# Rounding of one expert's down weights placed behind the router's scores and the sorted list of experts

## The chip, the cores and the metric

The kernel runs on one core of a Trainium2 chip. The metric is the device time of that core in microseconds (us), as the median of several executions. Engines carry the profile's names: PE is TensorE, PEld its weight load, DVE is VectorE, ACT is ScalarE, POOL is GpSimd and SP is SyncE, which here only issues transfers.

## The reference

One layer of a diffusion backbone: 512 latent tokens and 256 context tokens of width 1024 pass a gated linear attention mixer; then a mixture of 16 experts follows, of which every token takes two. Cut to the part that matters here:

```
x = x + g1 * y                                   # y: the mixer's output
h2 = modulate(rmsnorm(x, norm2_g), sh2, sc2)
scores = sigmoid(h2 @ w_router); sel = scores + b_router
# the best of 4 groups of 4 experts (by its two highest), and in it the top 2 experts
gates = one_hot(top2) * scores / sum(scores of the two)
for e in range(16):
    he = silu(h2 @ w1[e]) * (h2 @ w3[e])         # 1024 -> 512
    out = out + gates[:, e] * (he @ w2[e])       # 512 -> 1024, the "down" product
x = x + g2 * out; return rmsnorm(x, final_g)
```

All inputs are float32.

## The kernel before

A program orders each engine's instructions: a list scheduler takes the traced instructions by priority and readiness in a simulation, unless a block is marked as a manual schedule (those keep the written order among themselves, and others may be put between them). Inside `with tc.issue_after(i)` every instruction on i's engine is put behind i on that engine; it is an order on that queue, not a wait on another engine.

Around the change there are four stages. First, the mixer's output projection (`oproj` in `project(n)`, for four blocks of 128 tokens): float32 products as three fp32r products (`mm3`, lines 51 to 53) of a rounded part and a rest. `second(n)` adds the residual (lines 717 and 718) and squares (719), `turn` transposes a block on PE (725) and copies it (727), `logits` multiplies by the router (732). Second, the scores: `score` (854), `add_bias` (857), the sigmoid's exponential on ACT (904, named `scored`), its rest on DVE, then 11 filler products on PE (`warm`, 912) while DVE works out the top two (924 to 941, result `ohs`). Third, PE counts (943 to 947), DVE makes one-hot rows `hot` (956), and `collect` (964) multiplies them with the residual stream to gather the tokens of expert 0, which gets its first 128 tokens that way; meanwhile DVE sorts experts 2 to 15 by load (1042 to 1052, the last is `eidl`) and writes the normalised tokens to memory for the gathers of the others (`scaled`, `normed`, 839 and 842). This stretch up to `collect` is one manual schedule over DVE, ACT, POOL and PE. Fourth, the experts: 0 and 1 always run, the rest in the order of the sorted list. Expert 0's gate and up products (line 1181) use raw float32 weights; its down product goes through `conv`: ACT casts a 128x1024 tile of weights to fp32r (`S.copy`, line 56), DVE subtracts to get the rest (`V.tensor_sub`, line 57), and PE takes both. There are three pairs of buffers for such halves (`wh`/`wl` twice and `fx`), used in turn, so that the down product's four tiles take three pairs and then the first again. Expert 1's gate and up tiles (line 1256) already stand behind `scored` and `eidl`.

Weights of 1 MB a tile come by SP's queue (`load_unit`, line 688), each into the next free buffer; `release` hands a buffer back and `pump` issues the next load. Experts' tokens come by indirect transfers on POOL (1102) and results are added to memory by others (1106).

Of the kernel before, what the change touches and what calls it, by code (L numbers as in the profile page):

```python
# [32 lines left out]
def dit_kernel(ctx: ExitStack, tc: tile.TileContext, I, out):  # L33
# [21 lines left out]
    def split(hi, lo, full):  # L55
        S.copy(hi, full)  # L56
        return V.tensor_sub(lo, full, hi.bitcast(F32))  # L57
# [17 lines left out]
    cc = glt("cc", [2, 8])  # L75
# [200 lines left out]
    def conv(st):  # L276
        w = cvs.pop(0)
        cvs.append(w)
        if halves[0]:
            for k in range(2):  # L280
                S.copy(w[0][:, k], st[:, k])  # L281
                mark[0] = V.tensor_sub(w[1][:, k], st[:, k], w[0][:, k].bitcast(F32))  # L282
        else:
            mark[0] = split(w[0], w[1], st)
        return w
# [413 lines left out]
    def release(u, *us):  # L699
        free.extend(u.pop(s) for s in us)  # L700
        pump()
# [39 lines left out]
    for k2 in range(4):  # L741
        w = first[k2] if k2 < 2 else wconv(2 * k2)
# [11 lines left out]
    w = [wconv(8), wconv(10)]  # L754
# [149 lines left out]
    scored = [S.activation(sc, lg, AF.Exp, scale=-1.0)]  # L904
# [334 lines left out]
    class Expert:  # L1239
# [32 lines left out]
        def down(s, u):  # L1272
            s.turn()
            for kt in range(4):
                w = u[4 + kt // 2][:, kt % 2 * D:kt % 2 * D + D]
                if not s.raw:
                    ws = conv(w.rearrange("p (a n) -> p a n", a=2))
                for t in s.tls:
                    t.dn(kt, w if isinstance(t, Part) else ws)
                if kt % 2:  # L1280
                    release(u, 4 + kt // 2)
            if s is not ex[0]:
                s.store()
# [112 lines left out]
    with tc.manual_schedule(engines={G.engine}):  # L1396
        ex = [Expert(cols[order[0]], True)]
# [23 lines left out]
    with tc.manual_schedule(engines=tail):  # L1421
        p_, q_ = ex[NE - 2:]
        p, q = p_.tls[0], q_.tls[0]
# [69 lines left out]
    n = nc.values_load(nblk[0:1, 0:1], min_val=0, max_val=NB)  # L1493
# [46 lines left out]
```

## Time and profile before

| what | value |
|---|---|
| median of 3 runs | 656.51 us (656.42 to 659.3) |
| profiled execution, its own time | 656.5 us |
| its span, first to last instruction | 654.7 us |
| PE busy | 599.0 us (91%) |
| DVE busy | 463.6 us (71%) |
| ACT busy | 302.6 us (46%) |
| transfers | 168.41 MB, mean 257 GB/s |

1.8 us of the profiled execution lie outside its span. A busy PE is not a PE at its peak: the row on the granted clock tells whether it ran at 2.4 or at 1.2 GHz.

### The profile page before, as it was taken

The page shows a single profiled execution, that of the slowest core. Times are in us where ns is not written, and L with a number is a line of the kernel's source. Part 1 is how long each engine was busy: PE and PEld are TensorE (multiplying, and loading weights), DVE is VectorE, ACT ScalarE, POOL GpSimd, SP SyncE. Part 2 cuts the span into 40 slices and gives each one's busy share as a digit, 9 for nine tenths or more (in the row PEclk, how much of TensorE's full clock was granted, in tenths as well). Part 3 has the DMA queues.
Part 4 walks back from the last instruction along what each step waited for, and adds up shares of the span by engine and source line. Part 5 has one row for each costly group of instructions (what it writes and reads, how often), then busy time and mean ns, then how long its engine had stood idle before and what let it go on. Part 6 is the DMA issues. An engine that isn't in the chain of part 4 may idle for free. (4 is left out here: it accounts for less than half of the span.)

```text
span 654.7 us, 11203 instructions
## 1 busy us (share of the span) xinstructions
PE 599.0 (91%) x4200; PEld 412.4 (63%) x4200; DVE 463.6 (71%) x984; ACT 302.6 (46%) x511; POOL 98.3 (15%) x102
## 2 busy tenths in 40 slices
PE   3999999999999999999979989999999999999741
PEld 2778577776878878778748465545565657664310
DVE  5667499849985972575288399465767689999615
ACT  6433399257352233642451255334444457773131
POOL 4030000010100010012200330120322222222032
PEclk9999999999999999999998999999999999999975
DMA  8996472220234861658662989899999999999974
GB/s 269 340 353 218 175 274 66 67 66 4 67 130 158 270 232 51 254 183 354 237 227 74 373 316 366 326 342 351 412 387 395 362 352 358 393 383 345 298 273 189
DMA packets 50251, 168.41 MB, mean 257 GB/s; under 512 B 6779, under 2 KB 17237, under 8 KB 37138
## 3 DMA queue, kind: packets, MB, share of 16 engines
q1 hardware_dynamic: 43216, 156.26, 64.4%
q0 software_dynamic: 5024, 8.70, 5.6%
q10 hardware_dynamic: 1954, 2.71, 1.3%
q8 instruction: 34, 0.56, 0.3%
q14 instruction: 23, 0.19, 0.1%
HBM read 158.64 MB, written 12.30 MB: 261 GB/s over the span
## 5 line engine op out<-in xcount | busy, mean ns | idle before, releaser
L51 PE MATMUL bk<-wh,fh 128*128 128x512 f32 (+3 forms) x276 | 110.9, 409 | 0.7 <-ACT fh L56 0.4
L52 PE MATMUL bk<-wl,fh 128*128 128x512 f32 (+3 forms) x276 | 111.3, 405 | 0.0
L53 PE MATMUL bk<-wh,fl 128*128 128x512 f32 (+3 forms) x276 | 109.0, 399 | 0.5 <-DVE fl L57 0.5
L282 DVE TENSOR_TENSOR wl<-st,wh 128x512 fp32r<-128x512 f32 x60 | 39.9, 685 | 38.9 <-ACT wh L281 37.6
L56 ACT CAST wh<-su 128x1024 fp32r<-128x1024 f32 x45 | 46.8, 1047 | 39.9 <-PE bk L53 38.7
L281 ACT CAST wh<-st 128x512 fp32r<-128x512 f32 x60 | 35.9, 620 | 59.5 <-PE bk L53 50.8
L51 PEld LDWEIGHTS bk<-wh,fh 128*128 128x128 f32 (+3 forms) x276 | 50.2, 183 | 19.2 <-ACT wh L56 3.3
L57 DVE TENSOR_TENSOR wl<-su,wh 128x1024 fp32r<-128x1024 f32 x45 | 54.5, 1222 | 10.5 <-ACT wh L56 8.3
L1106 POOL DMA_INDIRECT accd<-y,gix x16 | 37.2, 2324 | 164.8 <-DVE y L1166 78.2
L52 PEld LDWEIGHTS bk<-wl,fh 128*128 128x128 f32 (+3 forms) x276 | 50.6, 183 | 16.5 <-issue 3.3
L53 PEld LDWEIGHTS bk<-wh,fl 128*128 128x128 f32 (+3 forms) x276 | 50.6, 183 | 13.7 <-issue 1.2
L1202 PE MATMUL bk<-su,he 128*64 128x512 f32 (+1 forms) x136 | 21.7, 526 | 12.5 <-DMA su<-in_w_down_e_dram 9.6
L1202 PE MATMUL bk<-su,xg 128*32 128x256 f32 (+1 forms) x216 | 31.7, 485 | 1.5 <-DVE xg L1196 1.5
L56 ACT CAST fx<-su 128x1024 fp32r<-128x1024 f32 x21 | 22.0, 1050 | 21.8 <-PE bk L53 21.6
L57 DVE TENSOR_TENSOR fx<-su,fx 128x1024 fp32r<-128x1024 f32 x21 | 25.7, 1222 | 7.4 <-ACT fx L56 7.2
L51 PE MATMUL bk<-fx,fh 128*128 128x512 f32 (+3 forms) x68 | 27.9, 410 | 1.2 <-ACT fh L56 1.2
L52 PE MATMUL bk<-fx,fh 128*128 128x512 f32 (+3 forms) x68 | 27.3, 402 | 1.0 <-DVE fx L57 1.0
L53 PE MATMUL bk<-fx,fl 128*128 128x512 f32 (+3 forms) x68 | 26.6, 394 | 0.2 <-DVE fl L57 0.2
L1102 POOL DMA_INDIRECT xg<-h2d,gix x16 | 20.1, 1259 | 39.2 <-DVE pis L1005 15.1
L250 POOL DMA_DIRECT2D mrd<-mrow x8 | 3.8, 487 | 129.2 <-DVE mrow L248 129.2
L1202 PEld LDWEIGHTS bk<-su,he 128*64 128x64 f32 (+1 forms) x136 | 6.6, 127 | 24.4 <-DMA su<-in_w_down_e_dram 11.0
L57 DVE TENSOR_TENSOR fl<-bk,fh 128x512 fp32r<-128x512 f32 (+3 forms) x25 | 15.5, 634 | 7.5 <-ACT fh L56 5.5
(476 smaller groups left out, 1303.6 us busy)
## 6 DMA issues: line engine op xcount, KB each, us to landing
su<-in_w_up_e_dram SPq DMA_DIRECT2D x23, 1024.0 KB, 8.2
su<-in_w_down_e_dram SPq DMA_DIRECT2D x21, 1024.0 KB, 7.8
su<-in_w_gate_e_dram SPq DMA_DIRECT2D x19, 1024.0 KB, 8.3
st<-in_gla_w_in_dram SPq DMA_DIRECT2D x10, 1024.0 KB, 5.0
QQ<-in_w_mod_dram SPq DMA_DIRECT2D x5, 1024.0 KB, 10.8
st<-in_w_gate_e_dram SPq DMA_DIRECT2D x5, 1024.0 KB, 6.8
st<-in_w_up_e_dram SPq DMA_DIRECT2D x5, 1024.0 KB, 9.0
B<-in_w_mod_dram SPq DMA_DIRECT2D x4, 1024.0 KB, 5.1
```

The lines of the kernel that those rows point to most:

```text
L51: PE.matmul(o, ah, bh, start=first, stop=False)
L52: PE.matmul(o, ah, bl, start=False, stop=False)
L53: return PE.matmul(o, al, bh, start=False, stop=last)
L56: S.copy(hi, full)
L57: return V.tensor_sub(lo, full, hi.bitcast(F32))
L250: G.dma_start(mrd[4 * h_ + c4:4 * h_ + c4 + 1, :], mrow[32 * c4:32 * c4 + 1, :])
L281: S.copy(w[0][:, k], st[:, k])
L282: mark[0] = V.tensor_sub(w[1][:, k], st[:, k], w[0][:, k].bitcast(F32))
L1102: G.indirect_dma_start(out=xg, out_offset=None, in_=src, in_offset=bass.IndirectOffsetOnAxis(ap=idx, axis=0), bounds_check=n - 1, oob_is_e ...
L1106: G.indirect_dma_start(out=dst, out_offset=bass.IndirectOffsetOnAxis(ap=idx, axis=0), in_=y, in_offset=None, bounds_check=n - 1, oob_is_er ...
L1202: PE.matmul(o[s.w * a:s.w * a + s.w], l, r(a), start=first, stop=last, tile_position=(0, s.w * a))
```

## The change

Expert 0 is `ex[0]`. The four conversions of its down weights are now traced inside two `issue_after` blocks: the four casts on ACT stand behind `scored` (line 904) on ACT's queue, the four subtractions on DVE behind `eidl` (line 1052) on DVE's queue. Nothing else is edited.

```diff
             for kt in range(4):
                 w = u[4 + kt // 2][:, kt % 2 * D:kt % 2 * D + D]
                 if not s.raw:
-                    ws = conv(w.rearrange("p (a n) -> p a n", a=2))
+                    with ExitStack() as cc:
+                        if s is ex[0]:
+                            for i in [scored[0], eidl]:
+                                cc.enter_context(tc.issue_after(i.ins))
+                        ws = conv(w.rearrange("p (a n) -> p a n", a=2))
                 for t in s.tls:
                     t.dn(kt, w if isinstance(t, Part) else ws)
```

## Rows read from the trace of the kernel before

**Rows 1.** The page: granted clock in 40 slices; one costly group (busy, mean ns).

```profile
PEclk9999999999999999999998999999999999999975
...
L56 ACT CAST wh<-su 128x1024 fp32r<-128x1024 f32 x45 | 46.8, 1047 | 39.9 <-PE bk L53 38.7
```

**Rows 2.** PE's timeline: start, duration, then [idle before <- what ended it].

```profile
327.61 0.40 PE L53 MATMUL bk<-wh,fx 128*128 128x512 f32 x1
...
336.06 0.40 PE L53 MATMUL bk<-wh,fx 128*128 128x512 f32 x1
...
341.12 0.63 PE L725 MATMUL bk<-ident,srg 128*128 128x128 f32 x4 [3.72 <-DVE srg L718]
...
343.12 1.89 PE L854 MATMUL bk<-sel,he 128*128 128x16 f32 x8
344.85 4.81 PE L912 MATMUL bk<-fh 128*128 128x512 f32 x11
349.70 0.20 PE L943 MATMUL bk<-ohs,tri 128*128 128x64 bf16 x1
...
350.76 7.51 PE L964 MATMUL bk<-hot,srg 128*128 128x128 f32 x64
...
380.45 1.07 PE L1136 MATMUL bk<-ident,xg 128*128 128x128 f32 x8
```

**Rows 3.** DVE's timeline ahead of the scores.

```profile
328.04 0.69 DVE L717 TENSOR_TENSOR srg<-bk,g1b 128x512 f32<-128x512 f32 x1 [0.26 <-PE bk L53]
328.76 0.69 DVE L718 TENSOR_TENSOR srg<-srg,su 128x512 f32<-128x512 f32 x1
...
335.69 1.22 DVE L57 TENSOR_TENSOR wl<-su,wh 128x1024 fp32r<-128x1024 f32 x1
...
337.35 1.23 DVE L57 TENSOR_TENSOR fx<-su,fx 128x1024 fp32r<-128x1024 f32 x1
...
338.56 0.68 DVE L717 TENSOR_TENSOR srg<-bk,g1b 128x512 f32<-128x512 f32 x1
339.16 1.22 DVE L57 TENSOR_TENSOR wl<-su,wh 128x1024 fp32r<-128x1024 f32 x1
340.29 0.69 DVE L718 TENSOR_TENSOR srg<-srg,su 128x512 f32<-128x512 f32 x1
```

**Rows 4.** ACT's timeline: the sigmoid's exponential and what comes next.

```profile
345.32 0.26 ACT L904 ACTIVATE sc<-lg 128x64 f32<-128x64 f32 x1 [1.79 <-DVE lg L857]
354.74 1.51 ACT L967 ACTIVATE full<-bk,m2T 128x128 f32<-128x128 f32 x4 [9.16 <-PE bk L964]
```

**Rows 5.** DVE's timeline from the list's last instruction to expert 0's end.

```profile
355.52 0.18 DVE L1052 CAST eid<-eidf 128x14 int32<-128x14 f32 x1
...
365.53 0.69 DVE L991 TENSOR_TENSOR ohx<-iot,zp 128x512 bf16<-128x512 bf16 x1
372.40 0.69 DVE L1148 TENSOR_TENSOR he<-he,bk 128x512 f32<-128x512 f32 x1 [6.18 <-PE bk L1181]
```

**Rows 6.** Windows: length, each engine's busy time, clock, DMA share, GB/s.

```profile
341.00:343.00 2.00, 1.45 (x20) 0.78 (x20) 1.21 (x4) 1.22 (x4) 0.00 (x0) 0.86 0.99 346
347.00:349.00 2.00, 2.00 (x6) 1.52 (x6) 1.97 (x11) 0.00 (x0) 0.00 (x0) 0.50 0.22 94
349.00:351.00 2.00, 1.83 (x15) 0.91 (x13) 1.47 (x8) 0.00 (x0) 0.00 (x0) 0.93 0.00 0
382.00:386.00 4.00, 3.52 (x21) 2.54 (x21) 4.00 (x22) 0.93 (x2) 0.95 (x1) 1.00 0.58 238
560.00:580.00 20.00, 19.70 (x99) 13.06 (x98) 19.54 (x32) 15.07 (x18) 5.98 (x2) 1.00 1.02 388
```

**Rows 7.** DVE's timeline near the end: one operation beside POOL's, and alone.

```profile
636.24 2.18 DVE L1351 TENSOR_TENSOR su<-B,srg 128x1024 f32<-128x1024 f32 x1 [5.54 <-DMA su<-accd]
642.62 1.22 DVE L1351 TENSOR_TENSOR su<-su,srg 128x1024 f32<-128x1024 f32 x1
```

**Rows 8.** POOL's timeline: the gather of expert 1's tokens, behind the gates.

```profile
368.87 1.10 POOL L1102 DMA_INDIRECT xg<-h2d,gix  x1 [2.59 <-DMA h2d<-xg]
```

## Prediction, made before the result was known

> **What bounds the kernel now.** I read the page first, for where TensorE does not have its clock: the row of the granted clock has nines almost throughout, an 8 in the slice from 344 to 360 us, and less at the very end [rows 1]. The slice with the 8 is the stretch of the scores, where the change lies, so I read the timelines of the engines there, and last the windows, to see what limits the stages behind it.
>
> Before the scores PE runs the output projection without a pause, and its last product starts at 336.06. Then it has nothing until 341.12: a pause of 3.72 us, ended by the residual addition (line 718) on DVE [rows 2]. The reader is to see in DVE's timeline why: DVE is not late with that addition because its input is late. It is busy with three subtractions of 1.22 us (line 57), which belong to expert 0's down weights, and these are wanted only some 35 us later. They stand among the small steps of the last token block: one at 335.69, one at 337.35 ahead of the product of line 717, and one at 339.16 between line 717 and line 718 [rows 3].
>
> From there a chain with no slack leads to the experts: addition, transposes, router products, scores (343.12), bias, exponential (345.32), the choice of the top two on DVE, the counts on PE (349.70), the collecting of expert 0's tokens (350.76) [rows 2 to 4]. PE's filler products run from 344.85 for 4.81 us, that is to 349.66, and end just when the counts can start, so they cost nothing [rows 2].
>
> **What the change takes from the path.** The three subtractions and their three casts leave this stretch. In the second token block, where nothing is put between, the product of line 717 starts at 328.04 after a last product that began at 327.61, 0.43 us later, and line 718 follows at 328.76, 0.72 us after line 717 [rows 2, 3]. By that pattern the last block's line 717 starts at 336.06 + 0.43 = 336.49 in place of 338.56, which is 2.07 us; and line 718 follows 0.72 us later in place of 340.29 - 338.56 = 1.73 us, which is 1.01 us. Together 3.08 us, and everything that hangs on line 718 moves by it. DVE is free by then: from 335.69 to 338.56 it has 2.87 us, of which the two subtractions are 2.45, so other work is 0.42 us, which fits into the 0.80 us from 335.69 to 336.49 [rows 3].
>
> **What it adds elsewhere: the casts.** ACT has 9.16 us without work behind the exponential until PE's collecting is ready [rows 4]. Three casts of 1.05 us [rows 1] take 3.1 us of it. Cost: nothing. If that cover were gone, they would cost their 3.1 us; but it would have to shrink by 6 us first. The fourth cast goes into a buffer pair that the first tile's products must leave first, so it stays where it was, during the down product.
>
> **The subtractions.** They now stand behind the list's last instruction, at 355.52 [rows 5]. Between that and expert 0's result DVE has a hole: its last small step starts at 365.53 and the next at 372.40 waits 6.18 us for PE [rows 5]. Three subtractions are 3.67 us, so they fit with 2.5 us to spare even if all else comes first. In which order the scheduler puts them is open. If they go ahead of the writes of the normalised tokens, the gather behind these writes is at most 3.67 us late against the rest; it starts at 368.87 [rows 8], and PE takes up its rows at 380.45 [rows 2], 11.6 us later, so a delay of that size has room. I take nothing; the other bound is the whole 3.67 us, if they miss the hole.
>
> A row near the end shows what POOL does to such an operation: a 128x1024 DVE product of two SBUF tensors took 2.18 us while POOL ran the same operation beside it and 1.22 us alone [rows 7]. The gates run on POOL ahead of the gather at 368.87 [rows 8], in just the stretch to which the subtractions go. The rule that stands behind this row: the Trainium skill, "SBUF — State Buffer", section "Who interferes with whom", says that a DVE instruction with two SBUF inputs and a GpSimd instruction that reads SBUF exclude one another, and the trace agrees with it by 2.18 against 1.22 us. By the rule the subtractions would be the slower the more gates they meet, which is the third rival below; without it they cost nothing.
>
> **The clock.** The fall and the rise lie inside the stretch: in the window from 341 to 343 us the mean clock is 0.86, which puts the fall to half (1.2 GHz) at 343 - 2 x 0.14 / 0.5 = 342.44; from 349 to 351 it is 0.93, which puts the rise at 349.28 [rows 6]. What PE did before the fall was the pause of 3.72 us and some short products; before the rise 4.4 us of filler products without a pause [rows 2]. With the pause cut to some 0.6 us (3.72 - 3.08) the scores may run at 2.4 GHz: their 1.89 us [rows 2] would be halved at best, so this gains 0 to 0.9 us. But then the fillers would end sooner too, and PE would stand idle ahead of the counts: at full speed 4.81 us become about 2.4, so a pause of 2.4 us, or less if the scores gained nothing. If the clock falls in that pause, collecting (7.51 us at full clock) starts slow, and as the rise came after 4.4 us of steady work, half of these, 2.2 us, are lost at most. So the clock's term lies between +0.9 and -2.2 us. The pause with a fall behind it was 3.72 us and the new one is 2.4, nearer to that than to none, so I count with a fall, but as it would come after part of the collecting or be over in part of it, with the smaller share: +0.4 for the scores and -0.4 for the collecting, nothing in sum. Both ends are kept.
>
> **Does it reach the end?** The stages behind are held either by PE or DVE or by transfers, and all of them start from this chain. Right behind expert 0, from 382 to 386, DVE is busy all of the 4 us and transfers only 0.58 [rows 6]: the engines set the pace. Later, as from 560 to 580, transfers are at 1.02 and PE at 19.70 of 20 [rows 6]: both. The loads that fill this stage go into buffers that the collecting and expert 0 free, so they move forward with them. I see nothing in the expert stage that is tied to an earlier time, so the 3.1 us should last: 656.5 - 3.1 = 653.4 us, from the profiled execution's own time, which is the median too (656.51).
>
> **The rivals.**
>
> *Clock lost in collecting.* The new pause ahead of the counts brings the fall to the collecting. Price up to 2.2 us, so a gain of 0.9 to 2.2: 654.3 to 655.6. For it speaks that a fall did come here [rows 6]; against it that the work ahead of the pause is denser than before.
>
> *Subtractions too late (slower).* The scheduler puts them behind the steps that wait for expert 0's result at 372.40. Then the down product waits for the first of them, and the rest fall into the stretch where DVE is full [rows 6], so up to 3.67 us are paid. The point from which it decides is 3.1 us: if all three miss the hole, 656.5 - 3.1 + 3.7 = 657.1, slower than before; with some of the reordering's own loss up to 659. Against it: they are ready long before, and DVE sits idle for 6.18 us [rows 5].
>
> *POOL in the way.* By the doubled duration of [rows 7] three subtractions would take 3 x 2.18 = 6.54 us for a hole of 6.18: 0.4 us lost, 653.8. Against it: the gates are small tensors, and each subtraction would have to meet one that is as long as itself.
>
> *Gain absorbed.* The transfers, at 1.02 from 560 on [rows 6], set the end whatever PE does before, or a new order of instructions in the experts gives it back: 656.5. Against it: they wait for buffers that are freed earlier. The change cannot fail to act at all, since the order on the queue is fixed by it, unless other work fills the holes; I see none.
>
> *More than that.* The clock does not fall at all and the later stages order themselves better: 652.4 or less.
>
> **How the numbers follow.** Forecast, 652.4 to 654.2 around 653.4: 0.55. Clock lost: 0.14. Subtractions late: 0.09. POOL: 0.05. Absorbed: 0.09. More: 0.08. The range must leave out no more than two in ten: it goes from 652.0, which leaves half of the last case out, to 656.6, which leaves out the late case. 0.5% is 3.3 us, about what a measurement of this kernel can tell from no change, so the line lies at 653.2, just inside the forecast. Of the forecast a bit under half lies below it, 0.25; all of "more" is 0.08; and 0.05 is for sizes that I took too low in the other cases: 0.38 faster. Slower by over 0.5% is above 659.8, which only a bad new order of the later stages gives, on top of the late case (0.02) or in place of "absorbed" (0.04): 0.06. The rest, 0.56, is the same.
>
> **What would show it.** In the changed trace line 57 has no instruction between 335 and 345; PE's pause of 3.72 us is below 1; line 718 follows line 717 after 0.72 us; the exponential starts near 342.2 or up to 0.9 earlier; three casts lie right behind it on ACT; three subtractions lie between 352.4 and 369.3 on DVE; collecting starts near 347.7 and takes 7.5 us at full clock, up to 9.7 if the fall is there; line 1148 starts near 369.3, and the down product behind it has no wait for line 57. I am wrong if the down product waits for a subtraction, if collecting runs at 1.2 GHz for long, or if the 3 us are there at 369 and gone by 400.

## The result, and the profile after

The change makes the kernel a little faster: 653.35 us median (650.64 to 657.62, 20 runs) against 657.18 us (653.83 to 661.07, 20 runs), a ratio of 0.995 with a 95% interval of 0.9929 to 0.9971. By the ratio that is 3.3 us, between 1.9 and 4.7; the two medians themselves differ by 3.83.

The profiled execution of the changed kernel has a span of 655.1 us, 0.4 more than the one before. Whoever compares these two numbers alone would call the change a loss, so the traces are compared by stretches.

DVE's timeline of the changed kernel, at the last token block and then behind the sorted list:

```profile
337.66 0.69 DVE L717 TENSOR_TENSOR srg<-bk,g1b 128x512 f32<-128x512 f32 x1
338.39 0.69 DVE L718 TENSOR_TENSOR srg<-srg,su 128x512 f32<-128x512 f32 x1
...
353.00 0.17 DVE L1052 CAST eid<-eidf 128x14 int32<-128x14 f32 x1
...
358.41 1.22 DVE L57 TENSOR_TENSOR fx<-su,fx 128x1024 fp32r<-128x1024 f32 x1
...
361.67 1.19 DVE L57 TENSOR_TENSOR wl<-su,wh 128x1024 fp32r<-128x1024 f32 x1
362.78 0.98 DVE L1071 TENSOR_TENSOR big<-zk,perm 128x784 f32<-128x784 f32 x1
363.68 1.21 DVE L57 TENSOR_TENSOR wl<-su,wh 128x1024 fp32r<-128x1024 f32 x1
...
369.88 0.69 DVE L1148 TENSOR_TENSOR he<-he,bk 128x512 f32<-128x512 f32 x1 [2.77 <-PE bk L1181]
```

Line 718 follows line 717 after 0.73 us, where it took 1.73 [rows 3], and the three subtractions stand behind the list, among the steps of the ranking (line 1071 is one). The hole ahead of expert 0's result has shrunk from 6.18 us [rows 5] to 2.77: the work moved into it, and nothing of it is late.

PE's timeline of the changed kernel:

```profile
337.23 0.40 PE L53 MATMUL bk<-wh,fx 128*128 128x512 f32 x1
...
339.22 0.63 PE L725 MATMUL bk<-ident,srg 128*128 128x128 f32 x4 [0.66 <-DVE srg L718]
...
341.22 1.29 PE L854 MATMUL bk<-sel,he 128*128 128x16 f32 x8 [0.16 <-DVE he L895]
342.35 4.14 PE L912 MATMUL bk<-fh 128*128 128x512 f32 x11
347.19 0.19 PE L943 MATMUL bk<-ohs,tri 128*128 128x64 bf16 x1 [0.71 <-DVE ohs L941]
...
348.24 7.51 PE L964 MATMUL bk<-hot,srg 128*128 128x128 f32 x64
...
355.79 13.98 PE L1181 MATMUL bk<-su,full 128*128 128x512 f32 x32
...
371.96 0.50 PE L51 MATMUL bk<-fx,fh 128*128 128x512 f32 x1 [0.68 <-ACT fh L56]
372.30 0.39 PE L52 MATMUL bk<-fx,fh 128*128 128x512 f32 x1
...
377.94 1.07 PE L1136 MATMUL bk<-ident,xg 128*128 128x128 f32 x8
```

The first products of expert 0's down weights (371.96 and 372.30) follow each other without a wait for a subtraction. The same timeline of the kernel before, two rows that were not shown, and then the changed kernel's row that answers to the second:

```profile
358.31 13.98 PE L1181 MATMUL bk<-su,full 128*128 128x512 f32 x32
...
601.39 3.65 PE L1202 MATMUL bk<-srg,xg 128*64 128x512 f32 x16
```

```profile
599.02 3.65 PE L1202 MATMUL bk<-srg,xg 128*64 128x512 f32 x16
```

PE's pause of 3.72 us [rows 2] is 0.66. From the last projection product to expert 0's first product (line 1181) the changed kernel takes 355.79 - 337.23 = 18.56 us, the one before took 358.31 - 336.06 = 22.25: 3.69 us less. The 0.4 us of the two spans is the sum of four stretches: the profiled execution of the changed kernel came to the last projection product 1.17 us later, in code that the change does not touch (a second execution of the same program, below, came there at 335.35, 0.71 us earlier than the kernel before); then 3.69 gained; then 243.23 in place of 243.08 us to the row of line 1202, 0.15 lost; and 56.08 in place of 53.31 us to the end, 2.77 lost. The experiments show that only the 3.69 belongs to the change.

ACT's timeline of the changed kernel, with the three casts behind the exponential:

```profile
342.82 0.26 ACT L904 ACTIVATE sc<-lg 128x64 f32<-128x64 f32 x1 [1.42 <-DVE lg L857]
342.98 1.03 ACT L56 CAST fx<-su 128x1024 fp32r<-128x1024 f32 x1
343.91 1.99 ACT L56 CAST wh<-su 128x1024 fp32r<-128x1024 f32 x2
352.22 1.51 ACT L967 ACTIVATE full<-bk,m2T 128x128 f32<-128x128 f32 x4 [6.32 <-PE bk L964]
```

6.32 us of the 9.16 [rows 4] are still free behind them.

### The profile page after: what moved, and what is told of

It is laid out like the page before. It is cut to its first block, busy times and chain, and to the rows that moved or that the text cites. A ratio compares the mean times of both kernels' runs of the same rounds, so it can differ in the third digit from the quotient of the medians.

```text
span 655.1 us, 11203 instructions
## 1 busy us (share of the span) xinstructions
PE 597.5 (91%) x4200; PEld 410.9 (63%) x4200; DVE 463.5 (71%) x984; ACT 302.9 (46%) x511; POOL 101.2 (15%) x102
```

## The experiments

One table for all, read from PE's timelines of one profiled execution each. "To collecting" is from the start of the last projection product to the start of line 964; "collecting" is that line's duration; "experts" is from the first product of line 1181 to the row of line 1202 shown above; "rest" from there to the end of the span. The ratio is to the kernel before, timed on the same chip; its median was 657.08 to 657.50 us there.

| kernel | to collecting | collecting | experts | rest | median us | ratio (95%) |
|---|---|---|---|---|---|---|
| before | 14.70 | 7.51 | 243.08 | 53.3 | 657.18 | |
| changed | 11.01 | 7.51 | 243.23 | 56.1 | 653.35 | 0.995 (0.9929 to 0.9971) |
| changed, again | 11.19 | 8.24 | 243.05 | 52.5 | 653.42 | 0.9941 (0.9916 to 0.9966) |
| subtractions only | 11.22 | 8.24 | 243.23 | 54.6 | 653.84 | 0.995 (0.993 to 0.9969) |
| casts only | 14.39 | 8.41 | 243.15 | 55.0 | 657.37 | 1.0014 (0.9992 to 1.0036) |
| subtractions late | 11.09 | 8.56 | 246.35 | 51.2 | 656.24 | 0.9991 (0.997 to 1.0012) |
| three idle ones added | 15.62 | 7.51 | 243.24 | 53.0 | 657.32 | 0.9995 (0.9976 to 1.0014) |
| nine idle ones added | 23.26 | 7.51 | 243.21 | 54.7 | 665.69 | 1.0113 (1.0092 to 1.0134) |
| subtractions past the gates | 11.00 | 7.51 | 243.12 | 51.5 | 653.27 | 0.9935 (0.9912 to 0.9957) |
| no fillers | 11.22 | 8.27 | 243.18 | 54.8 | 655.02 | 0.9958 (0.9937 to 0.998) |
| more fillers | 11.00 | 7.51 | 243.20 | 52.5 | 653.34 | 0.9948 (0.9928 to 0.9967) |
| before, with fillers | 14.05 | 8.80 | 243.13 | 51.9 | 656.79, one execution | |

**The changed kernel again.**

> The changed kernel once more, beside the kernel before on one chip. Theory (three subtractions off the scores' chain, 3.1 us, and the scores at full clock, 0.6 us): from the last projection product's start to the start of collecting (line 964) 11.0 us, where the kernel before has 14.70; the time 3 to 4 us under the kernel before. Rival (transfers set the end, the gain stays inside): the same 11.0 us, but the time within 1 us of the kernel before.

It took 653.42 us, 3.9 us under the kernel before by the ratio, with 11.19 us to collecting. The rival, a gain that stays inside, is out. PE's timeline of this execution, from the counts on:

```profile
345.29 0.21 PE L943 MATMUL bk<-ohs,tri 128*128 128x64 bf16 x1 [2.25 <-DVE ohs L941]
...
346.54 8.24 PE L964 MATMUL bk<-hot,srg 128*128 128x128 f32 x64
```

Here collecting took 8.24 us, behind a pause of 2.25 us ahead of the counts; more on that below. The profiled execution of this run has a span of 650.4 us, of the same program as the 655.1 above; the rest behind line 1202 is 52.5 us in the one and 56.1 in the other. So the 2.77 us that the first profile lost there is a spread of that stretch and not the change's. Over all kernels the rest lies between 51.2 and 56.1 us, in no order that follows the edits.

**Only the subtractions moved.**

```diff
-                            for i in [scored[0], eidl]:
+                            for i in [eidl]:
```

> Only the subtractions behind the list; the casts stay in the projection as in the kernel before. Theory: the casts cost nothing where they were, so 11.0 us from the last projection product to collecting, and the time of the changed kernel within 0.5 us. Rival (the casts hold up ACT's copies and squares there, and part of the gain is theirs): 11.5 us or more.

11.22 us to collecting, where the changed kernel took 11.01 and 11.19, and 653.84 us. So the gain comes without moving the casts: where they stood in the projection they cost nothing that these numbers show.

**Only the casts moved.**

```diff
-                            for i in [scored[0], eidl]:
+                            for i in [scored[0]]:
```

> Only the casts behind the exponential; the subtractions are free to follow them, and the order of instructions puts them at three places of the top-two choice on DVE, ahead of the counts. Theory: what counts is that DVE's subtractions stand on the chain, wherever; the scores come 3.7 us earlier as in the changed kernel, the choice takes some 3 us longer, so 14 to 14.7 us from the last projection product to collecting and the time of the kernel before within 1 us. Rival (only the place ahead of the scores hurts, for its pause of PE): 11 to 12 us, and 2 us or more faster than before.

The time is that of the kernel before. DVE's timeline of this kernel shows the three subtractions in the choice of the top two:

```profile
344.34 1.22 DVE L57 TENSOR_TENSOR fx<-su,fx 128x1024 fp32r<-128x1024 f32 x1
...
346.88 1.22 DVE L57 TENSOR_TENSOR wl<-su,wh 128x1024 fp32r<-128x1024 f32 x1
...
348.30 1.22 DVE L57 TENSOR_TENSOR wl<-su,wh 128x1024 fp32r<-128x1024 f32 x1
...
350.38 0.23 DVE L941 SCALAR_TENSOR_TENSOR ohs<-rk,gr 128x64 bf16<-128x64 f32 x1
```

The scores come as early as in the changed kernel, and against the run that moved only the subtractions 14.39 - 11.22 = 3.2 us are lost again between them and the counts. So the half of the change that matters is the one on DVE, and its place must be behind the whole chain; behind the scores is not enough.

**The subtractions late.** They stand behind the subtraction that splits expert 0's own hidden rows, past the hole.

```diff
-                            for i in [scored[0], eidl]:
+                            for i in [scored[0], s.tls[0].fl0]:
...
-            split(s.hh, s.hl, pt)
+            s.fl0 = split(s.hh, s.hl, pt)
```

> The subtractions are put behind the one that splits expert 0's own hidden rows, so past the hole on DVE; casts as in the changed kernel. This is the prediction's slower rival made real. Theory: collecting starts as in the changed kernel (11.0 us), then the down product waits about 1.2 us for the first subtraction, and DVE, which is full behind it, pays 1.2 to 3.7 us in all; the time 1 to 4 us above the changed kernel. If the later stages have slack on DVE: under 0.5 us above it.

PE's timeline of this kernel, in the down product and at its end:

```profile
373.06 0.73 PE L51 MATMUL bk<-fx,fh 128*128 128x512 f32 x2 [0.68 <-ACT fh L56]
374.92 0.79 PE L52 MATMUL bk<-fx,fh 128*128 128x512 f32 x1 [1.12 <-DVE fx L57]
375.51 0.63 PE L53 MATMUL bk<-fx,fl 128*128 128x512 f32 x1
...
381.90 1.07 PE L1136 MATMUL bk<-ident,xg 128*128 128x128 f32 x8
```

and one of its windows (length, each engine's busy time, clock, DMA share, GB/s):

```profile
376.00:378.00 2.00, 2.00 (x6) 1.59 (x5) 1.13 (x1) 0.93 (x1) 0.00 (x0) 0.50 1.02 336
```

The down product waits 1.12 us for the first subtraction. Behind it the granted clock is at half, 0.50 in this window, and products of 0.40 us take up to 0.63; in the changed kernel it is 1.00 there. The experts' stretch is 246.35 us, some 3.2 more than in every other kernel, and the time is 656.24 us, 2.8 above the changed kernel. The slower rival costs what it was said to cost, 1 to 4 us, and takes the gain back, but only in part in the way that was said. From the start of the two products of line 51 to line 52 it takes 1.52 us more than in the changed kernel (1.86 against 0.34), which is the wait; from line 52 to line 1136 it takes 1.34 us more (6.98 against 5.64), and there the clock is low. Behind that only some 0.3 us are left for a full DVE.

**Idle subtractions added.** The changed kernel with subtractions of no use between lines 717 and 718 of the last block, three or nine (`k`); nothing reads their result.

```diff
-        V.tensor_mul(x1[:, n, sl], ps, g1b[:, sl])
+        V.tensor_mul(x1[:, n, sl], ps, g1b[:, sl]); [V.tensor_sub(cvs[1][1], *[f.rearrange("p (a n) -> p a n", a=2) for f in (a2b, sh2b)]) for _ in range(k if (n, hf) == (3, 1) else 0)]
```

> The changed kernel with three subtractions of no use (same form, 1.22 us each, other data) between lines 717 and 718 of the last token block. Theory (time on DVE at this place is all that counted): addition 3.67 us later, so about 14.7 us from the last projection product to collecting as in the kernel before, and its time within 1 us. Rival (the gain came from elsewhere, the order of casts or of the later stages): the time stays 2 us or more under the kernel before.

> The same with nine of them, 11.0 us. Theory (everything behind hangs on this chain): 22 us from the last projection product to collecting and the time 7 to 8 us above the kernel before, 11 above the changed kernel. Rival (transfers set the end and can catch up): 5 us or less above the kernel before.

DVE's timeline with nine:

```profile
336.90 11.28 DVE L717 TENSOR_TENSOR wl<-xg 128x1024 fp32r<-128x1024 f32 x9
348.10 0.68 DVE L718 TENSOR_TENSOR srg<-srg,su 128x512 f32<-128x512 f32 x1
```

Three bring the time of the kernel before back (0.9995), though they read and write other data. Nine take 11.28 us, cost 12.3 us to collecting against the changed kernel (23.26 - 11.01; the long pause takes PE's clock at the scores as well) and 12.3 us of time (665.69 - 653.35). Both are a little more than expected: 23.26 us where 22 was said, and 8.4 us above the kernel before (657.33 on that chip) where 7 to 8 was. To within what these times tell (6.0 to 8.8 us above the kernel before, for 23.26 - 14.70 = 8.56 us on the chain) a microsecond on this chain is a microsecond of the kernel, and no catching up by transfers can be seen. With three, "to collecting" is 0.9 us longer than before, where the same was expected. About half of it is the subtractions: in the kernel before only 3.08 of the 3.67 us lay on the chain, and nearly all of them do here (line 718 starts 4.69 us after the last projection product, 4.23 before). The other half is the clock: the transposes behind the longer pause of 4.19 us take 1.09 us, 0.63 before.

**The subtractions past the gates.** They stand behind the last step of the ranking, line 1074 (`zpl` holds it).

```diff
-                            for i in [scored[0], eidl]:
+                            for i in [scored[0], zpl[0]]:
```

> The changed kernel with the subtractions behind the last step of the ranking on DVE (line 1074), inside the hole and past the gates on POOL. Theory (their place behind the list is covered): POOL's gates take the 5.1 us of the kernel before in place of the 7.1 us of the changed one, nothing waits for them, and the time is that of the changed kernel within 0.5 us. Rival (the meeting with POOL cost the change something): 1 us or more under the changed kernel.

POOL's timeline of the changed kernel:

```profile
358.64 1.31 POOL L1078 TENSOR_TENSOR big<-oh,sc 128x128 f32<-128x128 f32 x1 [42.04 <-DVE oh L1065]
...
361.83 1.10 POOL L1085 TENSOR_TENSOR gate<-big,wsum 128x8 f32<-128x8 f32 x1 [0.29 <-DVE wsum L1084]
...
363.89 1.07 POOL L1090 TENSOR_TENSOR gate<-gate,gsp 128x8 f32<-128x8 f32 x1
...
366.49 1.60 POOL L1102 DMA_INDIRECT xg<-h2d,gix  x1 [0.73 <-issue]
```

and of the kernel with the subtractions past the gates:

```profile
357.68 0.46 POOL L1078 TENSOR_TENSOR big<-oh,sc 128x128 f32<-128x128 f32 x1 [42.02 <-DVE oh L1065]
...
360.63 0.20 POOL L1085 TENSOR_TENSOR gate<-big,wsum 128x8 f32<-128x8 f32 x1 [0.29 <-DVE wsum L1084]
...
361.16 0.20 POOL L1090 TENSOR_TENSOR gate<-gate,gsp 128x8 f32<-128x8 f32 x1
...
364.97 1.43 POOL L1102 DMA_INDIRECT xg<-h2d,gix  x1 [1.76 <-DMA h2d<-xg]
```

In the changed kernel three POOL steps that take 0.2 to 0.5 us alone take 1.1 to 1.3, each begun just behind a subtraction on DVE (358.41, 361.67 and 363.68 above). Past the gates these three are short again; only the last cast of the gates still takes 1.08 us, at 362.12, behind the first subtraction at 361.94. The gates take 5.5 us in all, 7.1 in the changed kernel and 5.1 in the kernel before. The time is the same (0.9935 against 0.995 and 0.9941, the intervals cover one another), so the meeting is real and nothing hangs on it: the gather is wanted by line 1136 at 377.94 in the changed kernel, 11 us after it starts.

**Fillers.** First none behind the scores (the line `warm(11)` left out of the changed kernel), then 15 with the subtractions past the gates (`warm(15)`), then the kernel before with 12 filler products in PE's pause:

```diff
-        pt = bank().rearrange("p (k t) -> p k t", k=4)
+        pf_ = bank(); pt = pf_.rearrange("p (k t) -> p k t", k=4); [PE.matmul(pf_, hhl[0][:, 0:P], hhl[0], start=k == 0, stop=k == 11) for k in range(12 if (n, hf) == (2, 1) else 0)]
```

> The changed kernel without the 11 filler products behind the scores. Theory (the clock's price in collecting is real, and the fillers are what kept it away): the granted clock is at 1.2 GHz in collecting for a part, which takes 8 to 15 us in place of 7.5, and the time is 1 to 4 us above the changed kernel. If the clock does not fall there: the time of the changed kernel within 0.5 us.

> The subtractions past the gates on POOL, as in the run before, and 15 filler products behind the scores in place of 11, to leave PE a shorter pause ahead of the counts. Theory (where the clock falls in that pause, collecting takes 8.2 us in place of 7.5): 0 to 0.7 us under the run with 11 fillers. If four more fillers hold up the counts: up to 1 us above it.

> The kernel before, with 12 filler products ahead of the last but one block of transposes, so that most of PE's pause of 3.72 us is filled; the subtractions stay. Theory (of the change's 3.7 us some 0.6 come from the clock at the scores, 3.1 from the subtractions): the scores' 8 products take 1.1 to 1.3 us in place of 1.89, and from the last projection product to collecting it is 14.1 us in place of 14.70. Rival (the clock has no part in it): 14.7 us. One profile decides; the time itself moves too little.

PE's timeline of the kernel before with its pause filled:

```profile
337.78 3.02 PE L722 MATMUL bk<-fh 128*128 128x512 f32 x12
...
344.15 1.06 PE L854 MATMUL bk<-sel,he 128*128 128x16 f32 x8 [0.16 <-DVE he L895]
...
351.15 8.80 PE L964 MATMUL bk<-hot,srg 128*128 128x128 f32 x64
```

The scores take 1.06 us in place of 1.89 [rows 2] and "to collecting" is 14.05 in place of 14.70, with the subtractions where they were: the clock's part at the scores is 0.65 us. In this execution collecting takes 8.80 in place of 7.51, so the clock's fall has only moved there, and more is lost than was gained.

No fillers: 655.02 us, 1.6 above the changed kernel, but with overlapping intervals. The clock did fall, but collecting takes 8.27 us, no more than the 8.24 of the changed kernel's second profile, which has its fillers. What the 11 fillers are worth stays open. 15 fillers: collecting takes 7.51, but so it does with 11 in the run to which it is compared, and the time is the same (653.34 and 653.27). It beats neither.

## Why the prediction was right

**The subtractions.** Forecast 3.08 us off the chain, from the pattern of another token block. (PE's pause of 3.72 us begins at 337.40 and not with the last product at 336.06, as the prediction has it; the sum does not use this.) Measured: line 718 comes 338.39 - 337.23 = 1.16 us after the last projection product started, and came 340.29 - 336.06 = 4.23 us after it [rows 2, 3], so 3.07 us. The two runs with half the change and the two with idle work show that this is the cause; no part of the casts in it can be seen.

**The clock at the scores.** Forecast +0.4 between 0 and 0.9; measured 3.69 - 3.07 = 0.62 in the changed kernel, and 0.65 in the kernel before with its pause filled.

**The clock in collecting.** Forecast -0.4 between 0 and -2.2; measured between 0 and -0.7 for the changed program: 7.51 us in its first profile, 8.24 in its second. The new pause ahead of the counts, forecast at 2.4 us or less, was 0.71 and 2.25. The rival of that name is not wrong, then, but happens in some executions, at a third of its highest price here and at half in the late run (8.56), whose order up to collecting is the same. The clock's two windows in the first profile of the changed kernel, and two of the second one:

```profile
341.00:343.00 2.00, 1.84 (x14) 1.69 (x11) 1.32 (x8) 0.45 (x3) 0.00 (x0) 0.72 0.98 260
...
345.00:347.00 2.00, 1.49 (x6) 0.98 (x5) 1.90 (x11) 0.90 (x1) 0.00 (x0) 0.92 0.55 234
```

```profile
343.00:345.00 2.00, 0.04 (x1) 0.00 (x0) 1.91 (x11) 1.00 (x2) 0.00 (x0) 1.00 0.60 254
345.00:347.00 2.00, 1.71 (x13) 1.34 (x13) 1.50 (x7) 0.00 (x0) 0.00 (x0) 0.51 0.00 0
347.00:349.00 2.00, 2.00 (x13) 2.00 (x13) 2.00 (x7) 0.00 (x0) 0.00 (x0) 0.63 0.03 8
```

In the first the fall, near 341.9, meets the end of the scores and the fillers, and the clock is back before the counts. In the second the clock stays full through scores and fillers, falls at 345.0 near the end of a pause of 2.25 us and is back near 348.5, so that the first 1.9 us of collecting are slow.

**The subtractions' new place.** Forecast at no cost, by the hole of 6.18 us; so it is, 2.77 us of it are left. The late run shows what the cover is worth, 3.2 us in the experts' stretch and 2.8 of time. The price of that rival, up to 3.67 us, came out by some luck: it was to come from the wait and a full DVE, and 1.3 us of it were the clock.

**POOL.** This is the point that was read the wrong way round. The prediction took from [rows 7] that the subtractions would be slower beside POOL; they kept 1.19 to 1.22 us, and POOL's steps waited. In [rows 7] POOL's operation had begun first (at 634.99, DVE's at 636.24); here DVE's had. The Trainium skill, "SBUF — State Buffer", section "Who interferes with whom", says that the order of issue decides which one blocks, and these rows agree: 1.31 us in place of 0.46 for the POOL step that began at 358.64, behind a subtraction of 358.41. In the kernel without fillers it is the other way: POOL's first step begins at 357.45 and the subtraction of 357.48 takes longer.

```profile
357.45 0.46 POOL L1078 TENSOR_TENSOR big<-oh,sc 128x128 f32<-128x128 f32 x1 [41.95 <-DVE gix L1018]
```

```profile
357.48 1.51 DVE L57 TENSOR_TENSOR fx<-su,fx 128x1024 fp32r<-128x1024 f32 x1
```

**To the end.** Forecast that all 3.1 us last, since each later stage hangs on the chain. Shown: the experts' stretch is 243.05 to 243.24 us in eleven of the twelve profiles, whatever came ahead of it, and nine idle subtractions cost their full length. The sum, 653.4 us, lies at the measured 653.35, and so close by luck: it starts from 656.51, the median of three runs, where twenty runs have 657.18, and takes off 3.1 us, where the medians differ by 3.83. The clock's terms, +0.6 and 0 to -0.7, were taken to cancel; they do so only where collecting is slow. From the last projection product to the end of collecting the first profile gains 22.21 - 18.52 = 3.69 us and the second 22.21 - 19.43 = 2.78 (the table's first two columns added), and 3.1 lies between.

## What to carry to other kernels

In this kernel the list scheduler put work that is wanted late and ready early into the short gaps of a dependent chain, where it is longer than the gap; three subtractions of 1.2 us cost 3.1 there. Look for such instructions on the engine that carries the chain, and put them behind the chain's last step on that engine, not behind its first. Compare two profiles stretch by stretch from a common instruction: here the spans said 0.4 us slower and the stretch that was changed 3.7 us faster.

## What the runs showed of the hardware

The same program kept or lost its clock in collecting from one execution to the next: 7.51 and 8.24 us for 64 products, with the fall at 341.9 in the one and 345.0 in the other. Ahead of the second fall PE had run 2.8 us of fillers and then paused for 2.25 us. The same pause did not always bring a fall. Five profiles have 2.76 to 2.78 us of eleven fillers and then a pause of 2.25 to 2.28 us ahead of the counts. In four of them the clock fell, and collecting took 8.24 to 8.80 us. In the fifth, with the subtractions past the gates, it stayed at 1.00 in every window from 341 to 357 us, and collecting took 7.51; PE's row and the window around that pause:

```profile
346.25 0.19 PE L943 MATMUL bk<-ohs,tri 128*128 128x64 bf16 x1 [2.26 <-DVE ohs L941]
```

```profile
345.00:347.00 2.00, 0.75 (x10) 0.48 (x9) 1.46 (x9) 0.00 (x0) 0.00 (x0) 1.00 0.09 37
```

What decides between the two was not tried.

PE's stretch through the experts repeats to 0.2 us in 243, while the 53 us behind it spread over 51.2 to 56.1. In that last stretch PE waits 9.25 us for the last expert's down weights in the first profile of the changed kernel and 6.15 in its second. Counted from the row of line 1202 these products start after 641.12 - 599.02 = 42.10 us in the first and 39.44 in the second, which is 2.66 of the 3.55 us between the two rests. That points to the landing of the last transfers as the main source of the spread, but it is not shown; what makes these land sooner or later was not tried.

```profile
641.12 1.08 PE L1202 MATMUL bk<-su,he 128*32 128x256 f32 x8 [9.25 <-DMA su<-in_w_down_e_dram]
```

```profile
637.31 1.08 PE L1202 MATMUL bk<-su,he 128*32 128x256 f32 x8 [6.15 <-DMA su<-in_w_down_e_dram]
```
